# Chunk-attention heads with q's high and low parts below one another and k's rows doubled, and the FFN norm's squares added on VectorE

## The chip, the cores and the metric

The kernel runs on one core of a Trainium2 chip. The metric is the time of one execution on the device in microseconds (us); several executions are made, and their median counts.

## The reference, cut to what matters

Two layers of a streaming encoder run over 512 tokens of width 1024. Each layer normalises x, projects it, and lets three groups of attention heads work side by side: 6 latent heads, 6 differential heads (two score maps each) and 4 chunk heads. Their outputs are concatenated, projected and added to x; a gated feed-forward part (FFN) with its own norm follows.

```python
def chunk_attention(h, rel_bias):              # CH_HEADS = 4, CH_HD = 64
    q, k, v = [t.reshape(B, nc, CHUNK, CH_HEADS, CH_HD) for t in jnp.split(h, 3, axis=-1)]
    kb, vb = band(k), band(v)
    s = jnp.einsum('bnqhd,bnkhd->bnhqk', q, kb) * (CH_HD ** -0.5)
    s = jnp.where(valid, s + bias, -jnp.inf)
    p = jax.nn.softmax(s, axis=-1)
    return jnp.einsum('bnhqk,bnkhd->bnqhd', p, vb)
...
    x = x + jnp.concatenate([o_mla, o_diff, o_ch], axis=-1) @ w_out[l]
    x = x + conv_ffn(rms_norm(x, ffn_norm[l]), ...)
```

## The kernel before

**Numbers in two parts.** TensorE multiplies in fp32r, which keeps fewer bits than float32. So each float32 operand is split into a high part (a rounded copy, made by ScalarE or VectorE) and a low part (the rest, by a subtraction on VectorE), and a product is made of three matmuls that add up in one PSUM bank: high by high, high by low, low by high. `split` makes the two parts; it leaves the choice of engine for the copy to a planner.

**Attention scores.** `softmax_rows` makes the scores of a head in four row blocks of 128 queries; block i needs the first 128 (i+1) keys, so its matmuls are 128, 256, 384 and 512 columns wide. It writes into one of two PSUM banks (`pss` in the profile), VectorE adds the bias and takes the minimum of each row (a custom instruction), ScalarE takes the exponential. The pairs of operands come from the caller. Latent heads have 128 rows of contraction (`three(q, k, 0, 128)`, three matmuls a block). Differential heads have 96 rows: their three products of 32 rows stand below one another (function `stack`, by DMAs on GpSimd's queue), one matmul a block. Chunk heads have 64 rows: two heads share a tile of 128 rows, and head h uses rows 64 (h mod 2) and on, in three matmuls a block:

```python
yield from softmax_rows(three(qt, kt, 64 * (h % 2), 64), lambda i: ..., -1.0, res, buf)
```

The rescaled probabilities are transposed on TensorE (`pspt`), split again, and multiplied with the values (`psav`).

**Projections.** `proj` runs the three matmuls per 128 rows of weights into one of three PSUM banks (`psproj`). `unit` makes an input projection; its `finish` multiplies with the norm's factor and splits. `qk_unit` is the one for q and k. The jobs `c0` and `c1` make q and k of two chunk heads each. The output projection runs as jobs `a0` to `a7` (the first six of eight tiles of heads, ahead of the chunk heads' outputs) and `b0`, `b1` (the last two tiles). After `b`, `add_to_x` adds a bank to x and frees it, and `gain_f.add` prepares the FFN norm: two parts of x times gain (ScalarE and VectorE), the square (ScalarE), and its addition into a sum, which is given to GpSimd:

```python
add_to_x(NB_OUT * t + n, acc)
gain_f.add(NB_OUT * t + n, pool)
```

**The order of the work.** Instructions aren't issued as written: every engine call goes through `Clock.issue`, which records it with a cost and its dependences. Which job, score block or product comes next is picked by a simulated clock from when its operands are ready, and at the end `Clock.emit` schedules the whole list anew. So every instruction has line 364 in the profile, and one changed cost or dependence moves others. Each engine runs its list in the order given.

Of the kernel before, what the change touches and what calls it, by code (L numbers as in the profile page):

```python
# [12 lines left out]
F32 = mybir.dt.float32  # L13
# [3 lines left out]
ALU = mybir.AluOpType  # L17
# [3 lines left out]
S = 512  # L21
# [10 lines left out]
CH_SCALE = 64 ** -0.5  # L32
# [7 lines left out]
RINGS_R, NR = {}, 0  # L40
# [11 lines left out]
    RINGS_R[f"vd{u}"] = [v[(3 + u) % 5]]  # L52
for u in range(2):
    RINGS_R[f"cq{u}"], RINGS_R[f"ck{u}"] = ([RINGS_R["kmla"][2 * u + n]] for n in range(2))
    RINGS_R[f"vc{u}"] = [v[1 + u]]
for n in range(6):
    RINGS_R[f"x{n}"] = RINGS_R["x"][n : n + 1]
# [20 lines left out]
OUT = (1, 4, 7)  # L78
LATE = dict(qk=0, qm=0.5, og=0, lat=0, po=-99, hp=0, hs=99, sc=-0.2, p1=-0.5, st=-1, w=4)

ORDER = "kv q0 q1 kr e0 v e1 u0 u1 u2 d0 d1 d2 e2 c0 c1 g0 g1 a0 a1 a2 a3 a4 a5 a6 a7 b0 b1"

HEADS = "m0 m1 m2 d0 d1 d2 c0 c1"

# [395 lines left out]
def encoder(ctx, tc, xT, pos_row, pos_col, wflat, small, lam, relx, cst, out):  # L480
# [45 lines left out]
    def pair(tag):  # L526
        return T(tag).rearrange("p (c n) -> p c n", c=2)
# [53 lines left out]
    def split(src, hi, lo):  # L581
# [5 lines left out]
            dve.tensor_copy(hi, src)  # L587
        dve.tensor_tensor(lo, src, hi.bitcast(F32), op=ALU.subtract)


    widths = [KD * S, GCOLS, S, L * NCOL, cst.shape[1], P, NB, NB, 1]
    names = "xa dist rope sma ct ident posq posq_i eps".split()
# [115 lines left out]
    class Gain:  # L708
# [43 lines left out]
        def finish(self, f):  # L752
            if self.rb is None:
                self.held.append(f)
            else:
                f()
# [51 lines left out]
    def three(qt, kt, r0, n):  # L808

        return [(qt[r0 : r0 + n, a, :], kt[r0 : r0 + n, b, :]) for a, b in ((0, 0), (0, 1), (1, 0))]  # L810
# [72 lines left out]
    def layer(l, gain_a):  # L883
# [49 lines left out]
                put_off.append(("ev", turn["ev"], work.later(lambda: max(clock.at(f), clock.bank("pt")), rest)))  # L933
            return unit(name, gain_a, finish, gate)

        def chunk_qk(u):
            gate = lambda: (1, 1, 1) in stacks if u else ("m", 2, 1) in scored
            return [qk_unit(f"cq_{u}", f"cq{u}", gate, imm=CH_SCALE), qk_unit(f"ck_{u}", f"ck{u}", gate)]

        def diff_qk(u):  # L940
            gate = lambda: (("m", 0, 1) in scored, ("m", 1, 1) in scored, (0, 1, 1) in stacks)[u]
# [126 lines left out]

        def chunk_head(h, qt, kt, buf, res):
            rbias = biases[h]  # L1070
            yield from softmax_rows(three(qt, kt, 64 * (h % 2), 64), lambda i: rbias[:, S - 128 * (i + 1) :], -1.0, res, buf)
            scaled(*res)
            if h + 2 < CH_H:
                biases.append(load_bias(h + 2))
# [69 lines left out]
        def run_b(t, w):  # L1144
            for n in range(NB_OUT):
                c = slice(128 * KB * n, 128 * KB * (n + 1))
                acc = yield from proj(og[KA:], (w[0][:, c], w[1][:, c]), [])
                add_to_x(NB_OUT * t + n, acc)
                gain_f.add(NB_OUT * t + n, pool)

        jobs = {}

        def job(name):
            kind, t = name[0], int(name[1:]) if name[1:].isdigit() else 0
            return {
                "c": lambda: chunk_qk(t),
                "d": lambda: diff_qk(t),
                "g": lambda: v_unit(f"cv_{t}", f"vc{t}", lambda: tailed[0] >= 6),
                "e": lambda: v_unit(f"dv{t}", f"vd{t}", lambda: t < 2 or (tailed[0] >= 2 and jobs["v"].done)),
                "k": lambda: rope_key() if name == "kr" else latent("ckv", fkv, 1, C_KVN, 128),  # L1160
                "q": lambda: latent(f"cq{t}", fcq, 2, C_QN, 256),
                "v": lambda: latent_values(jobs),
                "u": lambda: latent_qk(t, jobs),
                "a": lambda: output_a(t),
                "b": lambda: weights(l, f"ob{t}", lambda w: run_b(t, w), Job.set, lambda: len(og) == 8),
            }[kind]()
# [103 lines left out]
        def scores():  # L1270
            for n, (kind, u, j) in enumerate(heads):

                over = max((k + 1 for k in range(n) if bufs[k] in bufs[n] + "X" * (kind == "d")), default=0)
                need = [jobs[f"u{u}"]] if kind == "m" else jobs[f"{kind}{u}"][:2]
                yield lambda: 0.0 if all(b.done for b in need) and (kind != "d" or (u, j, 0) in stacks) and tailed[0] >= over else NEVER
                res = []
                if kind == "c":
# [249 lines left out]
```

## Time and profile before

| what | value |
|---|---|
| median of 3 runs | 1240.6 us (1240.38 to 1242.81) |
| the profiled execution | 1241.23 us, its span 1239.1 us |
| TensorE (PE), busy share of the span | 98% |
| VectorE (DVE) | 69% |
| ScalarE (ACT) | 57% |
| GpSimd (POOL) | 10% |
| mean granted TensorE clock | 0.995 |

A profile records one execution. The span runs from its first to its last instruction; the 2.1 us between span and time lie around it. PEld is TensorE's loading of weights, which goes on beside its matmuls. A bracket at the end of a timeline row is the idle time of the engine ahead of the row, and what ended it.

### The profile page before, as it was taken

What the parts mean: (1) busy time and instruction counts of PE and PEld (TensorE: products, weight loads), DVE (VectorE), ACT (ScalarE), POOL (GpSimd) and SP (SyncE); (2) the same over time, 40 slices, a digit from 0 to 9 for tenths busy, and PEclk for the clock granted to TensorE, in tenths of its full rate; (3) what the DMA queues carried; (4) which work ended last, traced back from release to release, by engine and by line L of the source; (5) the groups of instructions that cost most, each with busy time, mean ns of one, the idle gap of its engine ahead of it and who ended that gap; (6) DMA issues with size and microseconds to landing.
All of it is one profiled execution on the core that took longest, in us unless ns stands there. A gap on an engine that the chain in (4) does not pass through costs nothing.

```text
span 1239.1 us, 15626 instructions
## 1 busy us (share of the span) xinstructions
PE 1215.1 (98%) x5607; PEld 991.1 (80%) x5607; DVE 861.0 (69%) x1596; ACT 704.2 (57%) x1233; POOL 123.0 (10%) x181
## 2 busy tenths in 40 slices
PE   8999999999999999999999999999999999999996
PEld 5788887788888888888877888777888888888885
DVE  7798997588774357665457889976876633677643
ACT  6797996765443234444477899876544422444432
POOL 0214310130000000000011143003100000000000
PEclk9999999999999999999999999999999999999998
DMA  5848961733322332323477498436333233332232
GB/s 169 188 104 186 227 134 43 166 103 122 102 87 82 104 105 100 102 81 91 127 163 163 100 235 175 93 79 151 103 102 102 77 97 116 102 96 91 79 97 79
DMA packets 51613, 146.33 MB, mean 118 GB/s; under 512 B 6480, under 2 KB 9552, under 8 KB 51536
## 3 DMA queue, kind: packets, MB, share of 16 engines
q1 hardware_dynamic: 37280, 106.27, 28.1%
q0 software_dynamic: 14256, 39.07, 17.5%
q8 instruction: 44, 0.72, 0.2%
q14 instruction: 33, 0.27, 0.1%
HBM read 132.21 MB, written 2.10 MB: 108 GB/s over the span
## 4 chain that ended last, share of the span: by engine, by line
PE 92%; DVE 3%; ACT 2%; DMA 2%; issue 1%; SPq 0%; DVEq 0%; ACTq 0%; POOLq 0%
PE psproj L364 80%; PE pss L364 5%; PE pspt L364 4%; PE psav L364 3%; DVE af L364 1%; DVE ar L364 1%; DMA ar<-in_wflat 1%; ACT ar L364 1%; ACT af L364 1%; DVE xa L364 1%; DMA xa<-in_xT 1%; DMA af<-in_wflat 0%; SPq L364 0%; ACT L880 0%; ACT rope L364 0%
## 5 line engine op out<-in xcount | busy, mean ns | idle before, releaser
L364 PE MATMUL psproj<-ar 128*128 128x512 f32 (+1 forms) x4595 | 1104.7, 392 | 8.3 <-DVE xa L364 2.2
L364 PEld LDWEIGHTS psproj<-ar 128*128 128x128 f32 x4595 | 849.3, 188 | 184.7 <-DVE ar L364 4.7
L364 ACT CAST ar<-af 128x512 fp32r<-128x512 f32 (+4 forms) x333 | 268.4, 820 | 219.8 <-PE psproj L364 195.7
L364 DVE TENSOR_TENSOR ar<-af,ar 128x512 fp32r<-128x512 f32 (+4 forms) x260 | 239.7, 925 | 145.3 <-PE psproj L364 79.3
L364 DVE SCALAR_TENSOR_TENSOR af<-af,sma 128x511 f32<-128x511 f32 (+1 forms) x192 | 141.9, 748 | 7.5 <-ACT af L364 4.9
L364 ACT ACTIVATE af<-af,sma 128x512 f32<-128x512 f32 x88 | 71.3, 816 | 121.2 <-DVE af L364 121.2
L364 DVE TENSOR_TENSOR af<-psproj,af 128x512 f32<-128x512 f32 x108 | 73.6, 686 | 61.4 <-PE psproj L364 61.0
L364 POOL DMA_DIRECT2D ar<-in_wflat x61 | 54.0, 886 | 617.8 <-ACT ar L364 601.0
L364 ACT ACTIVATE af<-af 128x512 f32<-128x512 f32 (+1 forms) x106 | 65.4, 622 | 71.6 <-DVE af L364 71.0
L364 ACT ACTIVATE af<-af,mn 128x128 f32<-128x128 f32 (+3 forms) x176 | 98.2, 559 | 7.4 <-DVE mn L364 7.0
L364 PE MATMUL pss<-ar 128*128 128x128 f32 (+7 forms) x336 | 88.1, 333 | 0.6 <-DVE mn L364 0.4
L364 PEld LDWEIGHTS pss<-ar 128*128 128x128 f32 (+2 forms) x336 | 56.6, 187 | 19.4 <-issue 7.7
L364 DVE TENSOR_TENSOR xa<-xa,psproj 128x512 f32<-128x512 f32 (+1 forms) x65 | 43.5, 674 | 40.4 <-PE psproj L364 40.3
L364 DVE TENSOR_TENSOR af<-af 128x512 f32<-128x512 f32 (+2 forms) x71 | 48.0, 677 | 33.4 <-ACT af L364 33.0
L364 DVE TENSOR_TENSOR ar<-pspt,ar 128x512 fp32r<-128x512 f32 (+1 forms) x106 | 63.2, 603 | 6.3 <-ACT ar L364 3.5
L364 PE MATMUL psav<-ar 128*128 128x512 f32 (+3 forms) x256 | 64.9, 331 | 0.3 <-DVE af L364 0.2
L364 PE MATMUL pspt<-ident,af 128*128 128x128 f32 x360 | 63.3, 275 | 0.3 <-DVE af L364 0.3
L364 ACT ACTIVATE ar<-af 128x1024 fp32r<-128x1024 f32 (+3 forms) x61 | 58.0, 950 | 8.0 <-PE psproj L364 5.6
L364 PEld LDWEIGHTS pspt<-ident,af 128*128 128x128 f32 x360 | 45.2, 140 | 14.4 <-DVE af L364 2.3
L364 PEld LDWEIGHTS psav<-ar 128*128 128x128 f32 x256 | 44.6, 189 | 8.8 <-issue 1.3
L364 ACT CAST ar<-pspt 128x512 fp32r<-128x512 f32 (+1 forms) x73 | 37.6, 524 | 17.1 <-PE pspt L364 15.5
L364 DVE CUSTOM_DVE_ANT_0 af<-pss,dist 128x384 f32<-128x384 f32 (+2 forms) x96 | 45.3, 484 | 2.9 <-PE pss L364 2.8
(67 smaller groups left out, 564.2 us busy)
## 6 DMA issues: line engine op xcount, KB each, us to landing
af<-in_wflat SPq DMA_DIRECT2D x125, 512.0 KB, 3.5
ar<-in_wflat POOLq DMA_DIRECT2D x37, 512.0 KB, 8.0
af<-in_wflat SPq DMA_DIRECT2D x48, 384.0 KB, 3.0
af<-in_wflat SPq DMA_DIRECT2D x38, 320.0 KB, 2.9
ar<-ar POOLq DMA_DIRECT2D x72, 128.0 KB, 6.2
ar<-in_wflat POOLq DMA_DIRECT2D x16, 384.0 KB, 6.2
xa<-in_xT SPq DMA_DIRECT2D x8, 256.0 KB, 6.8
af<-in_wflat SPq DMA_DIRECT2D x8, 256.0 KB, 3.8
```

The costliest lines, as they stand in the source:

```text
L364: self.clock.issue(self.name, op, outs, ins + aps, func, lambda: fn(*args, **kw))
```

## The change

For the chunk heads, q's tile now holds, for each head, the high part in the head's own 64 rows and the low part in the other 64. Of k there are two tiles (`ck` as before, and `cy`, in slots that `x` uses elsewhere): each holds one head's high part and low part in its own 64 rows, and a DMA on GpSimd's queue copies both into the other 64 rows. One matmul over 128 rows then gives (high q + low q) by high k, a second one (high q + low q) by low k: two matmuls a block in place of three. The job `c` makes q alone, and a new job `y` makes k; it may start once the differential heads' last stack is issued. The additions of the FFN norm's squares go to VectorE.

```diff
--- before.py
+++ after.py
@@ -52,6 +52,7 @@
     RINGS_R[f"vd{u}"] = [v[(3 + u) % 5]]
 for u in range(2):
     RINGS_R[f"cq{u}"], RINGS_R[f"ck{u}"] = ([RINGS_R["kmla"][2 * u + n]] for n in range(2))
+    RINGS_R[f"cy{u}"] = [RINGS_R["x"][u]]
     RINGS_R[f"vc{u}"] = [v[1 + u]]
 for n in range(6):
     RINGS_R[f"x{n}"] = RINGS_R["x"][n : n + 1]
@@ -78,7 +79,7 @@
 OUT = (1, 4, 7)
 LATE = dict(qk=0, qm=0.5, og=0, lat=0, po=-99, hp=0, hs=99, sc=-0.2, p1=-0.5, st=-1, w=4)
 
-ORDER = "kv q0 q1 kr e0 v e1 u0 u1 u2 d0 d1 d2 e2 c0 c1 g0 g1 a0 a1 a2 a3 a4 a5 a6 a7 b0 b1"
+ORDER = "kv q0 q1 kr e0 v e1 u0 u1 u2 d0 d1 d2 e2 c0 y0 c1 y1 g0 g1 a0 a1 a2 a3 a4 a5 a6 a7 b0 b1"
 
 HEADS = "m0 m1 m2 d0 d1 d2 c0 c1"
 
@@ -587,6 +588,13 @@
             dve.tensor_copy(hi, src)
         dve.tensor_tensor(lo, src, hi.bitcast(F32), op=ALU.subtract)
 
+    def high(src, hi):
+        n = hi.ap[-1][1]
+        if clock.through("act", 0.1 + n / 1200, src) < clock.through("dve", 0.07 + n / 1920, src) + LATE["hs"]:
+            act.copy(hi, src)
+        else:
+            dve.tensor_copy(hi, src)
+
 
     widths = [KD * S, GCOLS, S, L * NCOL, cst.shape[1], P, NB, NB, 1]
     names = "xa dist rope sma ct ident posq posq_i eps".split()
@@ -933,9 +941,33 @@
                 put_off.append(("ev", turn["ev"], work.later(lambda: max(clock.at(f), clock.bank("pt")), rest)))
             return unit(name, gain_a, finish, gate)
 
-        def chunk_qk(u):
-            gate = lambda: (1, 1, 1) in stacks if u else ("m", 2, 1) in scored
-            return [qk_unit(f"cq_{u}", f"cq{u}", gate, imm=CH_SCALE), qk_unit(f"ck_{u}", f"ck{u}", gate)]
+        def chunk_q(u):
+
+
+            def finish(job, acc, rb):
+                f = tmp("ev")
+                dve.scalar_tensor_tensor(f, acc, CH_SCALE, rb, op0=ALU.mult, op1=ALU.mult)
+                t = pair(f"cq{u}")
+                for j in range(2):
+                    own, other = slice(64 * j, 64 * j + 64), slice(64 - 64 * j, 128 - 64 * j)
+                    high(f[own, :], t[own, j, :])
+                    dve.tensor_tensor(t[other, j, :], f[own, :], t[own, j, :].bitcast(F32), op=ALU.subtract)
+                job.set(t)
+            return unit(f"cq_{u}", gain_a, finish, lambda: (1, 1, 1) in stacks if u else ("m", 2, 1) in scored)
+
+        def chunk_k(u):
+
+            def finish(job, acc, rb):
+                f = tmp("ev")
+                dve.tensor_tensor(f, acc, rb, op=ALU.mult)
+                ks = [pair(f"ck{u}"), pair(f"cy{u}")]
+                for j, t in enumerate(ks):
+                    own, other = slice(64 * j, 64 * j + 64), slice(64 - 64 * j, 128 - 64 * j)
+                    high(f[own, :], t[own, 0, :])
+                    dve.tensor_tensor(t[own, 1, :], f[own, :], t[own, 0, :].bitcast(F32), op=ALU.subtract)
+                    pool.dma_start(t[other, :, :], t[own, :, :])
+                job.set(ks)
+            return unit(f"ck_{u}", gain_a, finish, lambda: (2, 1, 1) in stacks)
 
         def diff_qk(u):
             gate = lambda: (("m", 0, 1) in scored, ("m", 1, 1) in scored, (0, 1, 1) in stacks)[u]
@@ -1068,7 +1100,7 @@
 
         def chunk_head(h, qt, kt, buf, res):
             rbias = biases[h]
-            yield from softmax_rows(three(qt, kt, 64 * (h % 2), 64), lambda i: rbias[:, S - 128 * (i + 1) :], -1.0, res, buf)
+            yield from softmax_rows([(qt[:, h % 2, :], kt[h % 2][:, n, :]) for n in range(2)], lambda i: rbias[:, S - 128 * (i + 1) :], -1.0, res, buf)
             scaled(*res)
             if h + 2 < CH_H:
                 biases.append(load_bias(h + 2))
@@ -1146,14 +1178,15 @@
                 c = slice(128 * KB * n, 128 * KB * (n + 1))
                 acc = yield from proj(og[KA:], (w[0][:, c], w[1][:, c]), [])
                 add_to_x(NB_OUT * t + n, acc)
-                gain_f.add(NB_OUT * t + n, pool)
+                gain_f.add(NB_OUT * t + n)
 
         jobs = {}
 
         def job(name):
             kind, t = name[0], int(name[1:]) if name[1:].isdigit() else 0
             return {
-                "c": lambda: chunk_qk(t),
+                "c": lambda: chunk_q(t),
+                "y": lambda: chunk_k(t),
                 "d": lambda: diff_qk(t),
                 "g": lambda: v_unit(f"cv_{t}", f"vc{t}", lambda: tailed[0] >= 6),
                 "e": lambda: v_unit(f"dv{t}", f"vd{t}", lambda: t < 2 or (tailed[0] >= 2 and jobs["v"].done)),
@@ -1271,7 +1304,7 @@
             for n, (kind, u, j) in enumerate(heads):
 
                 over = max((k + 1 for k in range(n) if bufs[k] in bufs[n] + "X" * (kind == "d")), default=0)
-                need = [jobs[f"u{u}"]] if kind == "m" else jobs[f"{kind}{u}"][:2]
+                need = [jobs[f"u{u}"]] if kind == "m" else jobs[f"d{u}"][:2] if kind == "d" else [jobs[f"c{u}"], jobs[f"y{u}"]]
                 yield lambda: 0.0 if all(b.done for b in need) and (kind != "d" or (u, j, 0) in stacks) and tailed[0] >= over else NEVER
                 res = []
                 if kind == "c":
```

TensorE's list holds 32 instructions fewer: 8 score matmuls less of each width, over 8 chunk heads (4 in each layer). VectorE's holds 14 additions of 128x512 more, 16 subtractions of 64x512 in place of 8 of 128x512, and 6 casts from `pspt` fewer; ScalarE's holds 16 casts of 64x512 in place of 8 of 128x512, and the 6 casts. GpSimd's holds 14 additions fewer and 8 DMAs of 64x1024 more.

TensorE, layer 0, chunk heads of the second pair, before (`pss_66` and `pss_67` are the two score banks, `psproj` projections, `pspt` transposes and a norm's sum, `psav` products with values):

```order
L364 MATMUL pss_66<-ar 128x128 x3
L364 MATMUL psproj_63<-ar 128x512
L364 MATMUL pspt_68<-ar,bones 128x512
L364 MATMUL psproj_63<-ar 128x512
L364 MATMUL psav_70<-ar 128x512
L364 MATMUL psproj_63<-ar 128x512
L364 MATMUL pspt_68<-ar,bones 128x512
L364 MATMUL pss_67<-ar 128x256 x3
L364 MATMUL psproj_63<-ar 128x512
L364 MATMUL psav_70<-ar 128x384 x2
L364 MATMUL psav_70<-ar 128x128
L364 MATMUL pspt_69<-ident,af 128x128
```

The same engine and stage after the change:

```order
L365 MATMUL pss_66<-ar 128x128 x2
L365 MATMUL psproj_64<-ar 128x512 x4
L365 MATMUL pspt_69<-ident,af 128x128 x2
L365 MATMUL psproj_64<-ar 128x512
L365 MATMUL pss_67<-ar 128x256
L365 MATMUL psproj_65<-ar 128x512
L365 MATMUL pss_67<-ar 128x256
L365 MATMUL psproj_63<-ar 128x512
L365 MATMUL psav_70<-ar 128x512 x2
L365 MATMUL psav_70<-ar 128x384
L365 MATMUL pss_66<-ar 128x384
```

The score blocks are two matmuls, together or with other work between them, and other work stands around them; of 64 or 128 rows the listing tells nothing.

VectorE, layer 1, from the output projection into the FFN, before (`xa<-xa,psproj` is `add_to_x` and frees a projection bank, `ar<-xa,sma,ar` the low part of x times gain):

```order
L364 TENSOR_TENSOR xa<-xa,psproj_65 128x512
L364 TENSOR_TENSOR ar<-af,ar 128x1024
L364 TENSOR_TENSOR xa<-xa,psproj_63 128x512
L364 SCALAR_TENSOR_TENSOR ar<-xa,sma,ar 128x512
L364 TENSOR_TENSOR xa<-xa,psproj_64 128x512
L364 SCALAR_TENSOR_TENSOR ar<-xa,sma,ar 128x512 x3
L364 TENSOR_TENSOR xa<-xa,psproj_65 128x512
L364 TENSOR_TENSOR xa<-xa,psproj_63 128x512
L364 TENSOR_TENSOR xa<-xa,psproj_64 128x512
L364 SCALAR_TENSOR_TENSOR ar<-xa,sma,ar 128x512
L364 TENSOR_TENSOR xa<-xa,psproj_65 128x512
L364 SCALAR_TENSOR_TENSOR ar<-xa,sma,ar 128x512 x3
```

The same place after the change (`af<-af` is the addition of a square):

```order
L365 TENSOR_TENSOR xa<-xa,psproj_63 128x512
L365 SCALAR_TENSOR_TENSOR ar<-xa,sma,ar 128x512
L365 TENSOR_TENSOR xa<-xa,psproj_64 128x512
L365 SCALAR_TENSOR_TENSOR ar<-xa,sma,ar 128x512
L365 TENSOR_TENSOR af<-af 128x512
L365 SCALAR_TENSOR_TENSOR ar<-xa,sma,ar 128x512
L365 TENSOR_TENSOR xa<-xa,psproj_65 128x512
L365 TENSOR_TENSOR af<-af 128x512
L365 SCALAR_TENSOR_TENSOR ar<-xa,sma,ar 128x512
L365 TENSOR_TENSOR xa<-xa,psproj_63 128x512
L365 TENSOR_TENSOR xa<-xa,psproj_64 128x512
L365 TENSOR_TENSOR af<-af 128x512
```

Before, three low parts in a row stood ahead of three additions to x. Now at most three other instructions stand between two of these additions, one of the three being a square's; three low parts in a row come later, when two of the three banks have been freed.

## Rows read from the trace of the kernel before

**Rows 1.** The page, busy us of each engine (share of the span) xinstructions.

```profile
PE 1215.1 (98%) x5607; PEld 991.1 (80%) x5607; DVE 861.0 (69%) x1596; ACT 704.2 (57%) x1233; POOL 123.0 (10%) x181
```

**Rows 2.** Waits of PE: what waited for whom, us, times, longest.

```profile
PE psproj L364 <- DVE xa L364: 2.2, 1, 2.2
```

**Rows 3.** Busy us by engine in stretches of both layers: span, PE, PEld, DVE, ACT, POOL.

```profile
112.50:184.80 72.30, 72.30 (x366) 59.96 (x366) 68.41 (x201) 68.97 (x162) 23.42 (x39) 1.00 0.88 189
184.80:221.80 37.00, 37.00 (x178) 25.77 (x176) 29.43 (x87) 25.88 (x63) 2.02 (x4) 1.00 0.24 54
...
716.00:788.40 72.40, 72.40 (x369) 60.18 (x368) 68.58 (x201) 68.59 (x162) 21.22 (x35) 1.00 0.82 174
788.40:825.30 36.90, 36.90 (x179) 25.94 (x178) 30.80 (x83) 25.59 (x62) 3.13 (x5) 1.00 0.36 80
```

**Rows 4.** Chain of work, latent heads (128 rows): start, us, what.

```profile
61.99 0.70 PE pss L364 x3
62.69 0.91 PE psproj L364 x4
...
77.80 0.28 PE pss L364 x3
...
79.23 0.36 PE pss L364 x3
...
80.56 0.53 PE pss L364 x3
```

**Rows 5.** Chain of work, chunk heads (64 rows), layer 0; first to last of 21.

```profile
183.85 0.48 PE pss L364 x3
...
204.02 0.48 PE pss L364 x3
204.50 0.43 PE psproj L364
...
206.08 0.55 PE pss L364 x3
206.63 0.43 PE psproj L364
...
207.59 0.72 PE pss L364 x3
...
210.06 0.89 PE pss L364 x3
...
219.33 0.89 PE pss L364 x3
```

**Rows 6.** Timeline of weight loads (PEld): a 96-row and a 64-row score.

```profile
133.02 0.19 PEld L364 LDWEIGHTS pss<-ar 96*128 96x128 f32 x1
...
206.01 0.41 PEld L364 LDWEIGHTS pss<-ar 64*128 64x128 f32 x3 [0.36 <-issue]
```

**Rows 7.** Timelines of DVE, POOL and PE, layer 1, start of the FFN.

```profile
857.33 0.75 DVE L364 SCALAR_TENSOR_TENSOR ar<-xa,sma,ar 128x512 fp32r<-128x512 f32 x1
...
858.59 4.57 DVE L364 SCALAR_TENSOR_TENSOR ar<-xa,sma,ar 128x512 fp32r<-128x512 f32 x3
...
857.58 5.03 POOL L364 TENSOR_TENSOR af<-af 128x512 f32<-128x512 f32 x3 [6.46 <-ACT af L364]
...
863.81 10.08 PE L364 MATMUL psproj<-ar 128*128 128x512 f32 x43 [2.21 <-DVE xa L364]
```

**Rows 8.** Groups by form: count, busy us, mean ns of one, idle before.

```profile
L364 DVE TENSOR_TENSOR af<-af 128x512 f32<-128x512 f32 x65 | 44.9, 690 | 33.3 <-ACT af L364 33.0
...
L364 DVE TENSOR_TENSOR ar<-af,ar 64x512 fp32r<-64x512 f32 x2 | 1.4, 690 | 0.1
...
L364 ACT CAST ar<-af 64x512 fp32r<-64x512 f32 x2 | 1.2, 618 | 0.4 <-DVE af L364 0.4
```

**Rows 9.** DMA issues: count, KB each, median us to landing.

```profile
ar<-ar POOLq DMA_DIRECT2D x6, 256.0 KB, 7.3
```

## The prediction, made before the changed kernel ran

> **What bounds the kernel now.** I read the page's shares first: TensorE is busy for 1215.1 of 1239.1 us, and no other engine for more than 861 [rows 1]. Then the waits: no single one of TensorE's is longer than 2.2 us, and one of these is for VectorE's addition to x [rows 2]. So almost every microsecond taken off TensorE's path is one off the span, as long as the other engines can follow. Whether they can is read by stage. From the first differential score to the first chunk score on VectorE (112.5 to 184.8 us, and 716.0 to 788.4), VectorE and ScalarE are busy for 95% beside a TensorE without a gap; from the first chunk score to the last (37.0 and 36.9 us), VectorE needs 29.4 and 30.8, ScalarE 25.9 and 25.6 [rows 3]. The change takes TensorE work out of that second stage, and VectorE has 7.6 and 6.1 us of idle time there: that room is what decides.
>
> **What one chunk score costs.** The chain of work shows three matmuls of 128 rows to take 0.28, 0.36, 0.53 and 0.70 us for 128, 256, 384 and 512 columns [rows 4], 1.87 us for the four blocks of a head. Of 64 rows the same three take 0.48, 0.55, 0.72 and 0.89 [rows 5], 0.19 to 0.20 more each, whatever the width. And the projection right behind takes 0.43 [rows 5] where one in a run takes 0.91/4 = 0.23 [rows 4]: another 0.20. The weight loads say why: ahead of the 64-row scores the loader stands idle for 0.36 us with "issue" as the reason, ahead of 96-row scores not at all [rows 6]; the load isn't done beside the matmul before it, but after it. So each excursion into 64 rows costs about 0.19 + 0.19 = 0.38 us (a transpose behind it pays somewhat less than a projection). There are 21 excursions in layer 0 (first and last in [rows 5]) and, counted in the same chain, 19 in layer 1, since some blocks are split by other work.
>
> The Trainium skill, TensorEngine Tiling (Array Packing), section Tiling Modes (Key Properties), says that a change of tiling mode drains TensorE; the rows agree with it, with 0.19 us on either side. Another page of the Trainium skill, TensorE: Matmul & The Clock Gate, section "Why this matters for your kernels", says that a single matmul of 32 rows takes as long as one of 128; it knows no price for going in and out, and by it only the third matmul would be saved. It is a rival below.
>
> **TensorE's gain.** 32 matmuls go, a third of 1.87 us in each of 8 heads: 8 x 0.62 = 5.0 us. The 40 excursions go, as the new scores have 128 rows like the latent heads': 40 x 0.38 = 15.2 us. Together 20.2 us, about 10 in each layer. This is the upper bound from TensorE's side. The lower bound, if excursions somehow remained, is 5.0.
>
> **What VectorE and ScalarE make of it.** The finish of each q and k job now makes two subtractions of 64x512 and two copies in place of one of each. A subtraction of 64x512 takes 690 ns and a copy on ScalarE 618, no less than for 128 rows [rows 8]: 8 x 0.69 = 5.5 us more on VectorE, 8 x 0.62 = 4.9 on ScalarE over both layers. Six casts go from VectorE to ScalarE by the planner's choice, which gives VectorE some 3.6 back. These finishes mostly stand in the stage ahead of the chunk scores, and its lists, priced by the mean of each shape (the kind of row of [rows 8]), change by -1.5 and +0.5 us on VectorE; TensorE's own there by -1.6 us in layer 0 (two projections and a few transposes and products moved on) and by nothing in layer 1. I take -1.2 and 0.
>
> In the chunk stage itself VectorE's list holds 71 and 68 instructions in place of 68 and 67, and priced the same way it is 3.2 and 1.6 us longer. Back to back, instructions overlap: traced busy time is 0.85 of that sum. So VectorE needs 29.4 + 2.7 = 32.1 and 30.8 + 1.3 = 32.1 us, while TensorE would need 37 - 10 = 27 plus what the order moves into the stage (8 and 3 projections at 0.23), some 28.5. VectorE now ends last. At 97% busy, a little above the 95% that it showed beside a busy TensorE [rows 3], the stage takes 33.0 us: a gain of 4.0 in layer 0 and 3.9 in layer 1. **So half of TensorE's gain turns into waits for VectorE.** Bounds: VectorE without any gap, 32.1 or a little less with tighter overlap (31), gives 4.8 to 6 each; VectorE with the utilisation of the stage before, 80 to 84%, gives nothing.
>
> Behind the last chunk score the chain to the output projection's last part (exponential, transposes, products, norm) is a latency with output projections as filler, and the projections moved ahead save little there: 0.5 in layer 0, 0.2 in layer 1.
>
> **The squares.** In layer 1 TensorE waits 2.21 us for an addition to x that frees a projection bank. It is queued behind three low parts that take 4.57 us, 1.52 each, while GpSimd adds squares for 5.03 us; one that starts before GpSimd takes 0.75 [rows 7]. Without GpSimd three would take 2.25, and the new order puts additions to x between them. I take the whole wait as gone: 2.2 us (bounds 0 and 2.2). The Trainium skill, SBUF — State Buffer, has a VectorE instruction with two inputs in SBUF share a port with GpSimd's reads, as an exclusive lock; the doubled time agrees, and nothing in the sum rests on it. Against this, VectorE gets seven additions of 0.69 us a layer [rows 8], 4.8 us, and gets back 3 x 0.77 = 2.3 us from those three alone. The norm's factor must be there when three projection banks are full, or TensorE waits; here I put 0.25 us a layer (bounds 0 and 1).
>
> **k's copies.** 8 DMAs of 256 KB more. Such a copy lands after 7.3 us [rows 9]; in the order, the shortest lead to its first score is 63 TensorE instructions, about 12 us. I cost them at nothing; a copy that landed 5 us later than the median would begin to show.
>
> **Sum.** Layer 0: 1.2 + 4.0 + 0.5 - 0.25 = 5.5. Layer 1: 0 + 3.9 + 0.2 + 2.2 - 0.25 = 6.0. Together 11.5 us. The profiled execution took 1241.2 us, its span 1239.1 and 2.1 around it; it becomes 1229.7. The median of the runs shown is 0.6 us below that execution: 1240.6 - 11.5, and I say 1229.
>
> **The rivals.** A change within 0.2% (2.5 us) can't be told from none.
>
> (a) Forecast: VectorE paces the chunk stage, gain 8 to 17 us, 1224 to 1233. Chance 0.62.
>
> (b) TensorE stays the bound, since VectorE's extra work is taken ahead or behind: 20.2 + 2.2 = 22.4 us at most, 1218; with small waits 1218 to 1224. For it: VectorE's list was made by a planner that put no price on excursions, so the order may be well spread. Against: 32 us of VectorE work between the first and the last score. Chance 0.14.
>
> (c) Excursions don't count or come back: only the third matmul is saved, 5.0 us, 1235.6, or less with waits, to 1238. This is the mechanism by which a matmul of few rows costs what one of 128 does and nothing else. Against it: 0.43 in place of 0.23 behind every excursion [rows 4, 5]. Chance 0.13.
>
> (d) No difference to be measured, 1238.1 to 1243.1: chunk stages that stay at 37 us. Chance 0.05.
>
> (e) Slower, above 1243.1. VectorE and ScalarE now are both near full in the chunk stage and take turns in one chain (minimum, exponential, rescaling, split): if each waits for the other, utilisation falls, and TensorE stands behind both with only two score banks. At 80%, as before (29.4 of 37.0), the stage takes 40 us, 3 us longer than now in each layer: 1240.6 + 6 - 2.2 = 1244.4. The point from which it decides is about 81%. Against it: in the stage before, the same chain ran at 95% on both engines [rows 3]. Chance 0.06.
>
> Faster by over 0.2% are (a), (b) and (c): 0.89; the same 0.05; slower 0.06. The range of 8 in 10 reaches over (a) and most of (b) and (c): 1219 to 1236.
>
> **What would show it.** In the changed profile: score matmuls in the chain at 0.19, 0.24, 0.35 and 0.47 us for two, with projections of 0.23 behind them and no idle weight loader ahead of them; if 0.43 is still there, the excursions' step is wrong. The chunk stages on VectorE at about 33 us with TensorE waiting some 4 us in each, mostly for VectorE's minima, parts of transposes or what ScalarE makes from them; no such waits means (b). Low parts at 0.75 us at the start of the FFN in both layers, GpSimd idle there, and no wait for an addition to x in layer 1. The forecast fails high if k's copies or the stacks' DMAs hold up a first chunk score, and low if VectorE's list shrinks in time by more than it grows in count.

## The result: 1228.4 us, 1% faster, and the profile after

The changed kernel takes 1228.37 us (median of 4 runs, 1228.03 to 1229.81), the kernel before 1241.34 beside it on the same chip (4 runs, 1240.38 to 1242.81). The ratio is 0.9897, its 95% interval 0.988 to 0.9914: 13.0 us less. Forecast were 1229 in a range of 1219 to 1236. The profiled execution took 1228.3 us, its span 1226.5.

The page of the changed kernel: busy us (share of the span) xinstructions, and, from another part of it, the shares of the chain that ended last.

```profile
PE 1200.3 (98%) x5575; PEld 984.5 (80%) x5575; DVE 859.0 (70%) x1612; ACT 710.0 (58%) x1247; POOL 104.6 (9%) x175
...
PE 80%; DVE 8%; issue 4%; ACT 4%; DMA 2%; POOL 1%; SPq 0%; DVEq 0%; POOLq 0%; ACTq 0%
```

Against [rows 1] TensorE is busy for 14.8 us less, and the span is 12.6 shorter, so TensorE's idle time grew from 24.0 to 26.2. It is still at 98%, but the chain is no longer on it alone. The chain line of the kernel before:

```profile
PE 92%; DVE 3%; ACT 2%; DMA 2%; issue 1%; SPq 0%; DVEq 0%; ACTq 0%; POOLq 0%
```

The windows of the changed kernel that answer to [rows 3] (from the first differential score's minimum on VectorE to the first chunk score's, and on to the end of the last chunk score's; layer 0, then layer 1; columns as there):

```profile
110.66:182.00 71.34, 71.28 (x356) 57.84 (x355) 67.63 (x197) 68.45 (x161) 24.73 (x42) 1.00 0.89 186
182.00:214.53 32.53, 31.91 (x184) 26.76 (x183) 31.42 (x90) 30.40 (x73) 3.06 (x6) 1.00 0.45 105
710.85:783.09 72.24, 72.24 (x364) 59.31 (x363) 68.54 (x201) 69.46 (x164) 23.85 (x39) 1.00 0.88 188
783.09:814.86 31.77, 31.06 (x178) 26.00 (x177) 30.91 (x87) 29.78 (x70) 2.98 (x6) 1.00 0.42 96
```

The third row of [rows 3] starts 1.4 us ahead of the first differential score's minimum. Taken from the minimum, the two differential stages of before are

```profile
112.61:184.77 72.16, 72.16 (x366) 59.84 (x365) 68.38 (x199) 68.83 (x162) 23.31 (x39) 1.00 0.88 188
...
717.43:788.45 71.02, 71.02 (x362) 58.96 (x361) 67.26 (x200) 68.18 (x161) 20.34 (x34) 1.00 0.81 173
```

The chunk stages fell from 37.0 and 36.9 us to 32.5 and 31.8. VectorE is busy for 97% of both, ScalarE for 93 and 94%. TensorE shows a gap of only 0.62 and 0.71 us, and it does as many instructions there as before (184 and 178) although some 15 score matmuls are gone from each stage: other work has moved in.

TensorE's own rows in layer 0, matmuls and then weight loads (start, us, what, count), answer to [rows 5] and [rows 6]:

```profile
187.50 0.48 PE L365 MATMUL psproj<-ar 128*128 128x512 f32 x1
187.82 0.34 PE L365 MATMUL pss<-ar 128*128 128x128 f32 x2
187.99 0.68 PE L365 MATMUL psproj<-ar 128*128 128x512 f32 x2
```

```profile
187.47 0.19 PEld L365 LDWEIGHTS psproj<-ar 128*128 128x128 f32 x1
187.61 0.40 PEld L365 LDWEIGHTS pss<-ar 128*128 128x128 f32 x2
187.93 0.30 PEld L365 LDWEIGHTS psproj<-ar 128*128 128x128 f32 x2
```

The projection behind two score matmuls starts 0.17 us after the first of them, and the loader has no idle bracket. A record's duration runs into the next one's, so starts are what to subtract; gaps under some 0.15 us never show as idle. They add up, so TensorE's **lost time** is counted below from starts in the traces: from each matmul's start to the next one's, less what such a matmul takes inside a run of its kind (0.060, 0.120, 0.176 and 0.227 us for 128 to 512 columns, 0.109 for a transpose, 0.428 for the few float32 matmuls at the start).

| kernel | chunk stages us | lost time in them us | in the whole execution us |
|---|---|---|---|
| before | 37.0, 36.9 | 8.5, 7.8 | 48.0 |
| changed | 32.5, 31.8 | 3.1, 3.3 | 40.1 |
| `e3_rows128` | 29.5, 30.0 | 1.3, 1.2 | 35.9 |
| `e4_rows64` | 37.5, 36.6 | 7.9, 7.7 | 51.2 |
| `e5_third` | 30.4, 30.7 | 1.3, 2.4 | 35.2 |
| `e6_noscale_after` | 27.2, 25.7 | 1.2, 1.0 | 37.4 |
| `e11_rows128_squares` | 30.4, 31.3 | 1.4, 1.2 | 31.8 |

The kernels below the first two are the experiments that follow. In a second execution of the changed kernel (`e13_after_again`) the stages and the lost time in them came out the same, the lost time of the whole at 41.7 us.

### The profile page after: what moved, and what is told of

It is laid out like the page before. It is cut to its first block, busy times and chain, and to the rows that moved or that the text cites. A ratio compares the mean times of both kernels' runs of the same rounds, so it can differ in the third digit from the quotient of the medians.

```text
span 1226.5 us, 15606 instructions
## 1 busy us (share of the span) xinstructions
PE 1200.3 (98%) x5575; PEld 984.5 (80%) x5575; DVE 859.0 (70%) x1612; ACT 710.0 (58%) x1247; POOL 104.6 (9%) x175
## 4 chain that ended last, share of the span: by engine, by line
PE 80%; DVE 8%; issue 4%; ACT 4%; DMA 2%; POOL 1%; SPq 0%; DVEq 0%; POOLq 0%; ACTq 0%
PE psproj L365 74%; DVE af L365 4%; DVE ar L365 3%; PE pss L365 3%; PE pspt L365 2%; PE psav L365 2%; ACT ar L365 2%; ACT af L365 2%; DMA ar<-in_wflat 1%; DVE xa L365 1%; POOL ar L365 1%; DMA xa<-in_xT 0%; DMA af<-in_relx 0%; SPq L365 0%; DVE rl L365 0%
## 5 line engine op out<-in xcount | busy, mean ns | idle before, releaser
L365 ACT CAST ar<-af 128x1024 fp32r<-128x1024 f32 (+4 forms) x341 | 272.5, 815 | 221.0 <-PE psproj L365 193.6
L365 DVE TENSOR_TENSOR ar<-af,ar 128x512 fp32r<-128x512 f32 (+4 forms) x268 | 243.3, 910 | 149.8 <-PE psproj L365 81.9
L365 DVE TENSOR_TENSOR af<-af 128x512 f32<-128x512 f32 (+2 forms) x85 | 57.6, 678 | 32.6 <-ACT af L365 32.1
L365 PE MATMUL pss<-ar 128*128 128x256 f32 (+7 forms) x304 | 79.0, 327 | 1.0 <-DVE mn L365 0.7
L365 PEld LDWEIGHTS pss<-ar 128*128 128x128 f32 (+1 forms) x304 | 52.5, 189 | 12.8 <-DVE mn L365 4.5
L365 POOL DMA_DIRECT2D ar<-ar x86 | 45.6, 540 | 71.7 <-DVE ar L365 23.1
```

The lines of the kernel that those rows point to most:

```text
L365: self.clock.issue(self.name, op, outs, ins + aps, func, lambda: fn(*args, **kw))
```

## Experiments

The theory from the prediction: excursions into 64 rows are nearly all of TensorE's gain; once they are gone, VectorE and ScalarE pace the chunk stage. The rivals: the third matmul, or having fewer instructions, bears the gain; or TensorE is still the bound.

### Excursions alone: `e3_rows128`, and put back: `e4_rows64`

`e3_rows128` is the kernel before with its three matmuls over all 128 rows of the shared tiles. Its scores are sums of two heads; the order of instructions on every engine is that of before.

```diff
-            yield from softmax_rows(three(qt, kt, 64 * (h % 2), 64), ...
+            yield from softmax_rows(three(qt, kt, 0, 128), ...
```

> The kernel before, with one thing changed: the three matmuls of a chunk score run over all 128 rows of the shared tiles in place of the head's 64, so each score is the sum of two heads' scores (that part of the computation is changed). The order on every engine is the same as before, row by row; nothing else differs. Theory 1 (each excursion into 64 rows costs about 0.38 us of TensorE, 40 of them, 15.2 us): the chunk stages fall from 37.0 and 36.9 us to about 32, where VectorE's 29.4 and 30.8 us of work begin to hold; in all 9 to 10 us less, some 1231.5 us. Theory 2 (a 64-row matmul costs what a 128-row one does, and only the third matmul counted): no difference, 1240.6 to 1241.5 us.

Measured: 1227.47 us (1225.14 to 1229.21), before 1241.14; ratio 0.9894 (0.9875 to 0.9913), 13.7 us less. More than expected: this alone does what the whole change does. The chunk stages fell to 29.5 and 30.0 us, where VectorE's list was expected to hold them at about 32:

```profile
184.33:213.80 29.47, 29.47 (x177) 25.45 (x175) 27.99 (x84) 24.66 (x62) 2.02 (x4) 1.00 0.24 58
781.57:811.60 30.03, 30.03 (x179) 26.33 (x178) 28.53 (x83) 25.59 (x62) 2.87 (x5) 1.00 0.38 84
```

VectorE runs the same list in the same order, 84 and 83 instructions of it in these windows (87 and 83 before), and is busy for 28.0 and 28.5 us in place of 29.4 and 30.8 [rows 3]. So a busy time read in a stage that another engine paces is not yet what the engine needs.

`e4_rows64` is the changed kernel, in its order, with both matmuls cut to the head's own 64 rows (q's low part is left out).

```diff
-  softmax_rows([(qt[:, h % 2, :], kt[h % 2][:, n, :]) for n in range(2)], ...
+  softmax_rows([(qt[own, h % 2, :], kt[h % 2][own, n, :]) for n in range(2)], ...   # own: 64 rows
```

> The changed kernel, with its two matmuls of a chunk score cut to the head's own 64 rows (the product of q's low part is left out). The order on every engine is that of the changed kernel, row by row. Theory 1 (excursions cost 0.38 us each): some 20 excursions a layer come back, the chunk stages go from 32.5 and 31.8 us to about 37, in all 9 to 11 us more than the changed kernel: about 1238.5 us, although the third matmul is still saved. Theory 2 (rows don't matter, only the number of matmuls): the changed kernel's time, 1228.4 us.

Measured: 1238.61 us (1236.37 to 1241.02), ratio 0.9984 (0.9974 to 0.9994): 10.2 us of the 13.0 go back, with two matmuls and the order unchanged. The chunk stages are 37.5 and 36.6 us again, as expected; TensorE's list has 33 runs of 64-row matmuls there, so each costs 0.31 us. Both directions agree: rows per matmul, not their number, bear the gain.

### The squares alone: `e1_squares_only`, and the heads alone: `e2_heads_only`

`e1_squares_only` is the kernel before with the new addition of squares; `e2_heads_only` is the changed kernel with the old one.

```diff
-                gain_f.add(NB_OUT * t + n, pool)
+                gain_f.add(NB_OUT * t + n)
```

> The kernel before with only the FFN norm's squares added by VectorE. Theory 1 (the 2.2 us wait for an addition to x in layer 1 came of VectorE held up by GpSimd's additions): 2.2 us less, about 1238.7 us, all of it at the start of layer 1's FFN, and nothing in layer 0. Rival (seven more additions a layer, 4.8 us, make VectorE late for the norm's factor): no gain, or up to 2 us slower.

Measured: 1238.97 us, ratio 0.9986 (0.9976 to 0.9997), 2.2 less.

> The changed kernel with the FFN norm's squares added by GpSimd as before: the chunk heads' part alone. Theory 1 (the parts add up): about 10 us less than before, 1230.5 us, with a wait of about 2 us for an addition to x at the start of layer 1's FFN as before. Rival (the squares' 2.2 us were an accident of the order, and any new order loses the wait): 1228.4 us, as the changed kernel.

Measured: 1232.59 us, ratio 0.9935 (0.992 to 0.9951), 8.5 less. The parts, 2.2 and 8.5, fall 2.3 us short of the 13.0: behind the shorter heads the old squares cost 4.2 us, not 2.2. The intervals are too wide for so small a difference, but PE's waits in `e2_heads_only` (whom for: us, times, longest) point the same way. [rows 2] had one such wait, and the changed kernel has 0.9 us of them, none above 0.4; here 2.2 us stand at the start of layer 0's FFN and 1.6 at that of layer 1's:

```profile
PE psproj L365 <- DVE xa L365: 4.5, 4, 2.2
```

In the changed kernel, the low parts of x times gain in layer 1 (VectorE's timeline; compare [rows 7]) are

```profile
852.61 0.68 DVE L365 TENSOR_TENSOR af<-af 128x512 f32<-128x512 f32 x1
853.21 2.07 DVE L365 SCALAR_TENSOR_TENSOR ar<-xa,sma,ar 128x512 fp32r<-128x512 f32 x3
855.20 0.68 DVE L365 TENSOR_TENSOR xa<-xa,psproj 128x512 f32<-128x512 f32 x1
```

three in 2.07 us where they took 4.57 beside GpSimd's additions.

### The third matmul put back: `e5_third`

The changed kernel with its second score matmul made twice (q times the low part of k counts double).

```diff
-  ... for n in range(2)], ...
+  ... for n in (0, 1, 1)], ...
```

> The changed kernel with a third matmul of 128 rows in each chunk score block (the second one once more, so q by low k counts twice: that part of the computation is changed). TensorE's work grows by 5.0 us. Theory 1 (in the chunk stage VectorE paces, busy for 31.4 of 32.5 and 30.9 of 31.8 us, and TensorE has room): 0 to 2 us more than the changed kernel, 1228.5 to 1230.5. Theory 2 (TensorE is the bound there too): 5 us more, 1233.4.

Measured: 1227.4 us (1226.59 to 1228.17), before 1239.69; ratio 0.9899 (0.9884 to 0.9914), the changed kernel's own. The third matmul's removal, 5.0 us of TensorE's work, is worth nothing here. The order is planned anew, though, and the stages are not those of the changed kernel:

```profile
110.66:184.08 73.42, 73.25 (x367) 59.68 (x366) 69.10 (x203) 70.25 (x165) 24.98 (x41) 1.00 0.86 187
184.08:214.51 30.43, 30.43 (x182) 26.55 (x181) 29.03 (x86) 28.42 (x68) 2.04 (x5) 1.00 0.39 92
```

Its lists put more into the differential stage and less into the chunk stage. Counted by starts, the 32 matmuls add 4.7 us of work, and TensorE loses 4.9 us less over the whole execution.

### Less work for VectorE and ScalarE: `e6_noscale_after`, `e7_noscale_before`

The rescaling of the chunk heads' probabilities is left out, in the changed kernel and in the kernel before.

```diff
-            scaled(*res)
+            pass
```

> The changed kernel without the rescaling of the chunk heads' probabilities by their sums (that part of the computation is left out): 32 row scalings on VectorE and ScalarE of 0.28 to 0.71 us go, some 7 us a layer over both engines. Theory 1 (VectorE and ScalarE pace the chunk stage): the chunk stages fall by 1.5 to 3 us each, to the 29 or so that TensorE needs, some 1223 to 1225.5 us in all. Theory 2 (TensorE is the bound): 1 us or less, 1227.5 to 1228.4.

Measured: 1226.23 us (1225.47 to 1228.37), ratio 0.9893 (0.9878 to 0.9907): the time missed what VectorE's pace would give and can't be told from the changed kernel's. But the stages themselves fell, to 27.2 and 25.7 us (windows as above):

```profile
181.58:208.76 27.18, 27.18 (x160) 23.23 (x159) 25.82 (x76) 25.64 (x64) 3.47 (x7) 1.00 0.54 123
...
781.76:807.42 25.66, 25.66 (x155) 22.06 (x154) 24.34 (x70) 24.02 (x60) 1.83 (x4) 1.00 0.37 83
```

TensorE does 24 and 23 instructions fewer in them. At the 0.23 us that a projection takes, that is 5.5 and 5.3 us, and the stages fell by 5.3 and 6.1: what had stood in the stage as filler is done behind it. There layer 0 takes 3.6 us more up to the next layer's first score, layer 1 4.8 more to its end. TensorE's lost time in the stages falls to 1.2 and 1.0 us.

> The kernel before without the rescaling of the chunk heads' probabilities (left out: the multiplication of each block by its row factor; the sums of the outputs are then not normalised). Theory 1 (TensorE with its 64-row excursions paces the chunk stage of the kernel before): VectorE's and ScalarE's lists get shorter, the two chunk stages stay at 36 to 37.5 us each, the time within 1.5 us of before (1239 to 1242). Rival (VectorE's and ScalarE's chain already paced the stage of before, so that the change's gain there is not TensorE's): the chunk stages fall by 3 us or more each, as they did by 5.3 and 6.1 us in the changed kernel, and the time to 1236 or less.

Measured: 1236.28 us (1233.2 to 1240.1), ratio 0.9967 (0.9955 to 0.9978). The stages are

```profile
184.13:223.85 39.72, 39.72 (x198) 28.49 (x197) 31.29 (x80) 28.03 (x65) 2.88 (x5) 1.00 0.26 58
...
791.42:826.44 35.02, 35.02 (x172) 24.73 (x172) 27.45 (x71) 23.95 (x58) 0.99 (x4) 1.00 0.21 48
```

together 74.7 us where 73.9 were: no fall, as theory 1 had it, with TensorE busy throughout (198 and 172 instructions in place of 178 and 179). The time, 4.1 us less, missed its range. The order is another one there, and the 2.2 us wait for an addition to x is absent from PE's waits; where the rest comes from was not settled.

The chain that ended last, through the chunk stage of layer 0 (shares of that window, by engine and line), before, after and after without rescaling:

```profile
by line: PE psproj L364 36.2%; PE pss L364 29.8%; PE psav L364 16.8%; PE pspt L364 16.7%; ACT ar L364 0.8%; issue 0.1%
```

```profile
by line: ACT af L365 28.5%; ACT ar L365 20.1%; DVE af L365 19.6%; issue 15.0%; DVE ar L365 12.6%; POOL ar L365 5.2%; DVE rl L365 0.7%; DVE mn L365 0.5%; POOLq L365 0.1%
```

```profile
by line: PE psproj L365 45.6%; PE pspt L365 19.1%; PE pss L365 18.0%; PE psav L365 17.9%
```

The second one must not be read as the pace of the chunk scores. That chain leaves TensorE behind the stage, at 237.75 us, where an output projection waits 0.99 us for the low part of a weight; it goes back along GpSimd's queue, which brings that part, and from there through ScalarE and VectorE. Without that wait TensorE's own chain is at most 1 us shorter. In layer 1 the same happens at 838.32 us, with another result, and in the second execution, where that wait is absent, the chain is mostly TensorE's (the changed kernel, then `e13_after_again`):

```profile
by line: issue 42.5%; DVE af L365 28.3%; DVE ar L365 16.9%; DMA af<-in_relx 7.8%; POOL ar L365 5.3%; DVE rl L365 1.0%; DVE mn L365 0.7%; POOL af L365 0.5%; POOLq L365 0.2%
```

```profile
by line: PE psproj L365 30.3%; DVE af L365 12.3%; PE pspt L365 11.1%; PE pss L365 9.9%; ACT af L365 9.5%; ACT ar L365 8.3%; PE psav L365 8.2%; DVE ar L365 7.4%; issue 4.1%; DVE rl L365 0.5%; DVE mn L365 0.3%
```

### What the finishes cost: `e9_padded_q`, `e10_k_by_dma`, `e12_k_by_dma_third`, `e11_rows128_squares`, `e13_after_again`

`e9_padded_q` gives k back its one tile and its old finish, and puts q into two tiles with zeros in the other head's rows: three matmuls of 128 rows.

```diff
+                    pool.memset(t[other, :, :].bitcast(F32), 0.0)
                     high(f[own, :], t[own, 0, :])
                     dve.tensor_tensor(t[own, 1, :], f[own, :], t[own, 0, :].bitcast(F32), op=ALU.subtract)
...
+  softmax_rows([(qt[h % 2][:, m, :], kt[:, n, :]) for m, n in ((0, 0), (0, 1), (1, 0))], ...
```

> Three matmuls of 128 rows: q stands in two tiles, one for each head, with its high and low part in the head's own rows and zeros in the other 64; k is made as before, one tile for both heads, with no copies by DMA. Squares on VectorE. Against the changed kernel TensorE has 32 matmuls (5.0 us) more, VectorE 4 subtractions (2.8 us) less, ScalarE 4 copies less. Theory 1 (the 128 rows are the gain, the third matmul is worth little, VectorE paces): 1 to 3 us less than the changed kernel, 1225.5 to 1227.5. Theory 2 (TensorE is the bound): 5 us more, 1233.

Measured: 1226.81 us (1225.6 to 1227.38), ratio 0.9896 (0.988 to 0.9913): the changed kernel's ratio, without the 5 us more of theory 2.

`e10_k_by_dma` is the changed kernel with k split once over 128 rows and spread by three DMAs in place of two.

```diff
-                for j, t in enumerate(ks):
-                    own, other = ...
-                    high(f[own, :], t[own, 0, :])
-                    dve.tensor_tensor(t[own, 1, :], f[own, :], t[own, 0, :].bitcast(F32), op=ALU.subtract)
-                    pool.dma_start(t[other, :, :], t[own, :, :])
+                split(f, ks[0][:, 0, :], ks[0][:, 1, :])
+                for rows in (slice(64, 128), slice(0, 64)):
+                    pool.dma_start(ks[1][rows, :, :], ks[0][64:128, :, :])
+                pool.dma_start(ks[0][64:128, :, :], ks[0][0:64, :, :])
```

> The changed kernel with k split over all 128 rows at once (one copy and one subtraction in place of two each) and three DMAs in place of two; the third overwrites rows that the first two read. VectorE has 4 subtractions (2.8 us) less, ScalarE 4 copies less, GpSimd's queue waits some 7 us for the first two copies, four times. Theory 1 (VectorE paces): 1 to 2.5 us less than the changed kernel, 1226 to 1227.4, unless the wait on GpSimd's queue makes weights late. Rival (the weights behind that wait come late): TensorE waits for weights, 0 to 5 us more.

Measured: 1223.0 us (1222.24 to 1225.52), ratio 0.9867 (0.9853 to 0.9882). It keeps the whole computation, and beats both kernels.

> The changed kernel with k split once over 128 rows and spread by three DMAs, and with the score's second matmul made twice (left wrong: q times the low part of k counts double). Theory 1 (the third matmul lies beside a full VectorE and ScalarE): as the version with two matmuls, 1223.0, range 1222 to 1224.5. Rival (with the lighter finishes TensorE ends last again, and pays 8 times 0.62 us): 1227 to 1228.5.

`e12_k_by_dma_third` (the diffs of `e10_k_by_dma` and `e5_third` together) took 1225.55 us (1225.07 to 1227.76), ratio 0.9881 (0.9864 to 0.9897): 2.5 us above `e10_k_by_dma` (1.7 by the ratios), between both theories. The intervals overlap, so a third to a half of the third matmul's 5.0 us is the best guess, not a finding.

> The kernel before with its chunk scores' three matmuls over 128 rows of the tiles as they are (scores are then sums of two heads) and the additions of squares on VectorE: everything that the change gains on excursions and squares, without the second k tile, the longer finishes and the third matmul's removal. Theory 1 (what is left out is worth nothing or costs): the two parts add up, 1227.5 - 2.2 = 1225.3, range 1223.5 to 1226.5, thus 2 to 4 us under the changed kernel. Rival (a common limit behind the chunk stages keeps every such version at the changed kernel's time): 1227 to 1229.

`e11_rows128_squares` (the diffs of `e3_rows128` and `e1_squares_only` together; scores are sums of two heads) took 1223.39 us (1221.7 to 1224.66), ratio 0.9858 (0.9844 to 0.9873): 17.0 us less than before, of the 15.2 + 2.2 = 17.4 that were forecast for excursions and squares at TensorE. Every engine runs the order of `e1_squares_only`, so this is the excursions' price a second time: 17.0 - 2.2 = 14.8 us, 0.37 each (15.9 by the ratios of the two groups of runs).

> The changed kernel once more, on the same chip as the others of this call, so that they can be compared: 1228, range 1226.5 to 1230; its early and differential stages (52.5, 71.3, 50.9, 72.2 us) differ by up to 1 us from those of the first execution.

The changed kernel beside it on the same chip (`e13_after_again`) took 1228.14 us (1226.92 to 1229.98), ratio 0.9899 (0.9884 to 0.9914). Its early and differential stages are 52.4, 72.5, 50.9 and 72.3 us; the second missed its 1 us by 0.1. The intervals of the two kernels lie apart: what the change does beyond excursions and squares, 32 matmuls saved and longer finishes, costs 4.8 us on balance.

Windows of `e11_rows128_squares` (its chunk stages), and its page:

```profile
183.53:213.92 30.39, 30.39 (x180) 26.20 (x179) 28.88 (x87) 25.52 (x63) 2.02 (x4) 1.00 0.26 62
...
780.57:811.87 31.30, 31.30 (x185) 27.38 (x184) 29.77 (x86) 26.55 (x64) 2.87 (x5) 1.00 0.40 91
```

```profile
PE 1202.7 (98%) x5607; PEld 991.5 (81%) x5607; DVE 856.7 (70%) x1610; ACT 703.1 (57%) x1233; POOL 100.5 (8%) x167
...
PE 91%; DVE 4%; ACT 2%; DMA 1%; issue 1%; SPq 0%; DVEq 0%; ACTq 0%
```

Its chain is on TensorE for 91%, as before the change. Its TensorE is busy for 2.4 us longer than the changed kernel's (0.7 longer than in that kernel's second execution) but idle for 20.2 us against 26.2 in both of those.

Four kernels with three matmuls of 128 rows and the squares on VectorE differ in how many finishes are split into 64-row halves, and with that in copies by DMA and in the planned order. Counted are the subtractions and copies beyond those of before; "PE's waits" is the sum of the rows of that view.

| kernel | subtractions, copies more | time us | ratio | PE's waits us |
|---|---|---|---|---|
| `e11_rows128_squares` | 0, 0 | 1223.39 | 0.9858 | 8.1 |
| `e12_k_by_dma_third` | 4, 4 | 1225.55 | 0.9881 | 8.9 |
| `e9_padded_q` | 4, 4 (and zeros by GpSimd) | 1226.81 | 0.9896 | 9.9 |
| `e5_third` | 8, 8 | 1227.4 | 0.9899 | 12.0 |

The count is read from the groups by form; in the changed kernel

```profile
L365 DVE TENSOR_TENSOR ar<-af,ar 128x512 fp32r<-128x512 f32 x98 | 67.1, 687 | 30.1 <-ACT ar L365 29.8
...
L365 DVE TENSOR_TENSOR ar<-af,ar 64x512 fp32r<-64x512 f32 x18 | 12.3, 683 | 0.6 <-ACT ar L365 0.2
...
L365 ACT CAST ar<-af 64x512 fp32r<-64x512 f32 x18 | 11.0, 614 | 1.3 <-DVE af L365 1.1
```

(8 of 128x512 fewer than before's 106, 16 of 64x512 more than [rows 8]'s 2). From the first row to the last, eight such pairs more go with 4.0 us more (5.1 by the ratios), about 0.5 each, where one takes 0.69 us of VectorE and 0.62 of ScalarE. Ratios of neighbours in the table overlap; those of the first and the last row don't.

## Why the prediction was right, and where it was not

**What bounds the kernel.** TensorE paced the chunk stage of before: with nothing changed but the rows of its matmuls (`e3_rows128`) the stages fell by 7.5 and 6.9 us, without rescaling (`e7_noscale_before`) they didn't shrink, and their chain is on PE.

**The excursions** bore the gain, as forecast. 40 x 0.38 = 15.2 us was the price; taken out in an unchanged order they give 13.7, or 0.34 each. In the order with the squares on VectorE they gave 14.8, or 0.37 each. The Trainium skill, TensorEngine Tiling (Array Packing), section Tiling Modes (Key Properties), has a change of tiling mode drain TensorE; `e3_rows128` and `e4_rows64` agree as to a price, with 13.7 and 10.2 us, while the drain itself is not seen in any run. The Trainium skill, TensorE: Matmul & The Clock Gate, section "Why this matters for your kernels", has a single matmul of 32 rows take as long as one of 128; by this alone both runs would have been no different from their partners. Rival (c) falls, and (d) and (e) with the 13.0 us.

**The third matmul** stood at 5.0 us in the upper bound of 20.2, and not in the sum, where VectorE ends the stage first. `e5_third` agrees with the sum: 0 in the changed kernel, perhaps 1.7 to 2.5 where finishes are lighter. Rival (b), TensorE as the bound at 1218 to 1224, falls for the changed kernel and describes `e10_k_by_dma` and `e11_rows128_squares` better.

**The chunk stage.** 33.0 us each were forecast, at 97% of VectorE; 32.5 and 31.8 came, at 97%. The sentence that failed is "So half of TensorE's gain turns into waits for VectorE", with some 4 us of waiting in each stage. As idle time 0.62 and 0.71 us show, which by the prediction's own sign would have meant rival (b). By starts TensorE loses 3.1 and 3.3 us there. Of these, 1.8 and 1.7 stand ahead of matmuls whose last semaphore came from VectorE no more than 0.1 us before they could have started, 0.1 ahead of those that ScalarE released, and the second execution has the same 1.8 and 1.7. In `e3_rows128` and `e11_rows128_squares` no such lost time is over 0.05 us a stage. So the waits are for VectorE, as stated, but at less than half of the forecast: of some 7 us that the excursions' end gives a stage they take back 1.8. The 97% alone doesn't show them: in `e3_rows128` VectorE is at 95% of a stage of 29.5 us. Other TensorE work fills the rest of the room, and a shorter stage by itself only hands that work on, as `e6_noscale_after` shows. What counts over the whole is TensorE's work plus its lost time. `e11_rows128_squares` has 4.7 us more of the one and 8.3 less of the other than the changed kernel; 3.8 of the 8.3 stand in the chunk stages, the rest is spread. PE's waits sum to 14.0 us in the changed kernel and 8.1 in `e11_rows128_squares`, none above 2.4. Two of them are new, 1.0 us in layer 0 and 1.1 in layer 1, for the low part of a weight in the output projection; in the second execution only the one in layer 0 is there. PE in layer 1:

```profile
827.51 9.69 PE L365 MATMUL psproj<-ar 128*128 128x512 f32 x42
838.32 23.94 PE L365 MATMUL psproj<-ar 128*128 128x512 f32 x103 [1.13 <-DMA ar<-in_wflat]
```

**The finishes** were priced at 5.5 us of VectorE and 4.9 of ScalarE, but on the path ahead of the chunk scores at -1.2 and 0. The differential stage came at -0.8 and +1.2. Over the whole kernel they took back about what the third matmul's removal gave, as the table of four shows.

**Behind the last chunk score** -0.5 and -0.2 were forecast. Layer 0 came at +0.9 up to the next layer's first latent score, layer 1 at -2.1 to the end, in which the squares' 2.2 stand.

**The squares.** The wait in layer 1 went whole: 2.2 us by `e1_squares_only`. Behind the new heads the old way would have cost more, 4.2 by the medians, since the wait appears in layer 0 too; that was not foreseen. The late norm factor, put at 0.25 us a layer, came at 0.19 and 0.16: at 269.23 and 869.51 us TensorE waits for the first multiplication with it on VectorE, which frees a projection bank.

**k's copies** cost nothing, as forecast: they land after 5.5 us, and PE's waits name none of them.

```profile
ar<-ar POOLq DMA_DIRECT2D x14, 256.0 KB, 5.5
```

**The sum** was 11.5 us, against 12.5 in the spans of the two profiled executions (13.0 in the medians). Set side by side:

| stretch | forecast gain us | came us |
|---|---|---|
| up to layer 0's first differential minimum | 0 | 2.0 |
| differential stages, layers 0 and 1 | 1.2, 0 | 0.8, -1.2 |
| chunk stages, layers 0 and 1 | 4.0, 3.9 | 4.5, 5.1 |
| from there to layer 1's first differential minimum | 0.25 | -0.7 |
| from layer 1's chunk stage to the end | 2.15 | 2.1 |

The last row bears the forecast out, and the chunk stages gave 1.7 more. That the total came within 1.5 us is luck in part: the differential stages gave 1.6 less, the stretch behind layer 0 0.9 less, and the first row, which no term had, 2.0 more. That row isn't to be counted as a gain: between its two executions the changed kernel itself differs there by 2.3 us (110.66 and 112.94).

**Open.** Only `e3_rows128`, `e4_rows64` and the step from `e1_squares_only` to `e11_rows128_squares` keep the order of their partners. Every other edit of the heads also changes the planned order, so the 4.8 us are shown for finishes and their order together; which instruction holds TensorE was not singled out. Single stages aren't read closer than the 1.1 us by which a differential stage differs between two executions.

## What to carry to other kernels

Look at what stands around a small matmul, not only at the matmul: a late start ahead of it and a late neighbour behind it priced each of these excursions at 0.34 us, more than the 0.28 that a block of three matmuls of 128 rows and 128 columns takes. When operands are rearranged to please TensorE, cost the rearranging at its full price on engines that are 95% busy, since halves of 64 rows take VectorE and ScalarE as long as 128 rows; one split over all rows with DMAs to spread it was 0.3% better here. And a shorter stage is a gain only as far as the bound engine loses less time: count the filler that moves, and count by starts, since most of the lost time here is in gaps too short to show as idle.

## What the runs showed of the hardware

Nothing but a use of rows changed in `e3_rows128`, and TensorE's 40 excursions turned out to cost 0.34 us each, while the 96-row scores beside them, of which the kernel holds 96, hardly show an idle loader ahead of them [rows 6]: at 2 of 89 places, against 32 of 40 ahead of 64-row scores. Three low parts that VectorE makes alone take 2.07 us, and 4.57 beside GpSimd's additions.
